# A two-norm transformer block on one core: the first pair of products written out by hand, with x turned by the host

## The chip, the cores and the metric

One core of one Trainium2 chip. A core has the engines PE (TensorE: matrix products, with its weight loads listed as PEld), DVE (VectorE: element by element), ACT (ScalarE), POOL (GpSimd) and SP (SyncE, which here only issues transfers), and 16 DMA engines that move data between HBM and the on-chip memory. The metric is device time in microseconds (us) of one execution; lower is better. All arithmetic on the data is in 32 bits.

## The reference

One layer on 512 tokens of width 2048, cut to what matters here:

```
h = rms_norm(x, norm1_g);  proj = h @ w_in         # columns qa ka va ra ga qb kb vb
A = chunked gated linear attention(qa, ka, va, gate from ga) ; out_a = rms_norm(A) * silu(ra)
B = dilated attention(rms_norm(qb), rms_norm(kb), vb)
x = x + concat(out_a, B) @ w_out
h2 = rms_norm(x, norm2_g)
x = x + (silu(h2 @ w_gate) * (h2 @ w_up)) @ w_down
```

## The kernel before

**Products.** All large products go by pairs: two weight blocks of 512 output columns are done together, as seven products P1 to P7 in place of eight (a scheme of sums and differences of quarters, as Strassen and Winograd do it). The left factor is the transposed x (or the transposed intermediate), in quarters r11, r21, r12, r22 of 256 features by 256 tokens; from them come the seven left operands A11, A12, A22, S1, S2, S3, S4. The right factor is in quarters named a, b, c, d; four products take a difference of two of them (`total` in the first pair, later `source`). Every operand is split into a high and a low part, since a product of full precision is made of three: ACT casts the high part (`wh`, `wl` is the low one, which DVE subtracts; for left operands `A...` the lines L174 and L175). A **unit** is one product for one group of 512 rows: 12 matrix instructions, 8 with `wh` and 4 with `wl`. A pair over 2048 rows is 28 units. There is one pair for qa and ka, four more on w_in, two on w_out, eleven on w_gate and w_up, six on w_down.

**The first pair** (`first_pair`, lines L384 to L492) differs from the rest. Nothing of x is on the chip when it starts. `LOADS` gives the order in which SP asks for x (16 pieces of 256 KB, rows as they lie in memory, `x_load`) and the weight quarters (512 KB each). PE turns x piece by piece (`x_turn`, L646: 64 transposes through `bank` in PSUM), and ACT (L658) or DVE (L653) scales the turned piece by the gain `g1` on its way into `xT`. The gains themselves arrive as rows and are turned by PE (`gains`, L566, L567), which needs the unit matrix `mats`. The lists `FIRST[i]` name what is put between the matrix instructions of unit i-2: `t` turns a piece, `+S1` to `+S4` add on DVE, `A..` and `S..` without a plus are splits, `sq` squares x on ACT for its norm (L621), `norm` finishes the norm, `gprep` makes the gate's weights from `gw` (POOL, ACT L735, DVE L736), `gate` are 32 of the gate's 64 small products (L753), and `seed` and `close` take a finished sum out of PSUM (L442 on ACT, L452 on DVE). A seed must be out before the next product adds to the same accumulator, and it needs the norm of x. The order on PE, ACT and DVE is exactly that of the program in this pair.

**The other pairs** come from `stream`. In each unit a `step` runs between the `wh` and the `wl` products: first what `later(n, ...)` has put off by n units, then one piece of the jobs in `background`. There the three engines' orders are set by a scheduler of the language from the order of the code, so neighbours may change places. A finished chunk of 512 columns is turned by `transposed_store` (PE L1071, ACT L1079 or L1082, then a store, L1086) and written to HBM: `mix_d` after the gate, `xn_d` after w_out, `p_d` after the gated product. The next stage loads it back by halves of 256 tokens (`part`, L1125; `fetch_part`, L1159). These buffers are laid out `[128, 2, 512]`, so that half a row is 1 KB.

Before the first pair on w_gate starts, A11 and S3 of all groups have to be in the program (`finish`). Groups 2 and 3 need the last chunks of w_out: `early_job` loads r11 and r21 of group 2 into `top`, splits A11, subtracts, splits S3, and then does the same for group 3.

A transfer that SP issues waits there for its data and for a free buffer, with all later transfers behind it.

## Time and profile before

| | |
|---|---|
| three runs | 1972.16, 1972.66, 1976.63 us; median 1972.66 |
| the profiled execution | 1970.3 us; its span, first to last instruction, 1968.5 us |
| busy, share of the span | PE 98%, PEld 85%, DVE 84%, ACT 55%, POOL 2% |
| moved | 294.49 MB read and 64.51 MB written, 182 GB/s over the span |
| mean granted PE clock | 0.997 |
| the first pair | 12.38 us (first product) to 105.30 us (first product of the next pair) |

Busy time is the union of an engine's instructions, so matrix instructions that overlap in the pipeline count once. The profile's rows give the start, the duration, the engine, the line, the operation, output and inputs, the count of merged instructions, and in square brackets how long the engine stood idle before it and who released it.

### The profile page before, as it was taken

How to read it: one execution, taken by the hardware profiler on the slowest of the kernel's cores; microseconds unless marked ns; L12 is line 12 of the kernel's file. 1: busy time of each engine (PE TensorE's matmuls, PEld its weight loads, DVE VectorE, ACT ScalarE, POOL GpSimd, SP SyncE). 2: the span in 40 equal slices, each digit the busy share in tenths (PEclk: the TensorE clock that was granted, in tenths of full speed). 3: DMA queues.
4: the chain of work that ended last, by engine and by line, in shares of the span. 5: the costliest groups of instructions: out<-in, count | busy, mean ns of one | idle time of the engine just before them, and what ended most of it. 6: DMA issues, size and time to landing. Idle time of an engine off the chain costs nothing.

```text
span 1968.5 us, 25771 instructions
## 1 busy us (share of the span) xinstructions
PE 1929.8 (98%) x9226; PEld 1669.3 (85%) x9226; DVE 1653.2 (84%) x1852; ACT 1086.9 (55%) x1586; POOL 47.4 (2%) x73
## 2 busy tenths in 40 slices
PE   7999999999999999999999999999999999999998
PEld 6888888888878878888888888888888888888887
DVE  7997778768789979878878878878879989989987
ACT  6664464566676656545545445545446646546443
POOL 0000130001000000000000000000000000000000
PEclk9999999999999999999999999999999999999999
DMA  7347364444566584443543453443545865855762
GB/s 278 113 174 270 103 203 151 150 163 159 191 225 213 189 273 161 171 172 128 179 169 134 172 171 124 172 167 126 176 166 164 288 211 180 302 180 181 243 214 75
DMA packets 183352, 358.34 MB, mean 182 GB/s; under 512 B 16070, under 2 KB 94735, under 8 KB 183224
## 3 DMA queue, kind: packets, MB, share of 16 engines
q1 hardware_dynamic: 183016, 356.62, 52.9%
q8 instruction: 72, 1.18, 0.2%
q14 instruction: 56, 0.46, 0.1%
q10 hardware_dynamic: 208, 0.08, 0.0%
HBM read 294.49 MB, written 64.51 MB: 182 GB/s over the span
## 4 chain that ended last, share of the span: by engine, by line
PE 71%; DVE 7%; DMA 4%; issue 2%; ACT 1%; SPq 1%; POOL 0%; DVEq 0%; ACTq 0%; POOLq 0%
PE acc L360 67%; DVE wl L334 2%; PE bank L1071 1%; DVE wa L255 1%; PE bank L956 1%; DMA k<-y_d 1%; PE bank L978 1%; DMA xn_d<-oT 1%; DVE AS L175 1%; ACT wh L330 0%; PE bank L971 0%; DVE seed L1249 0%; DVE seed L293 0%; PE bank L947 0%; DMA r<-mix_d 0%
## 5 line engine op out<-in xcount | busy, mean ns | idle before, releaser
L360 PE MATMUL acc<-wh,AS 128*128 128x512 f32 x3008 | 713.4, 380 | 1.8 <-DVE AS L175 1.0
L360 PEld LDWEIGHTS acc<-wh,AS 128*128 128x128 f32 x3008 | 567.7, 189 | 85.0 <-DVE AS L175 1.8
L330 ACT CAST wh<-wa 128x1024 fp32r<-128x1024 f32 x376 | 393.6, 1048 | 399.4 <-PE acc L360 367.6
L360 PE MATMUL acc<-wh,AA 128*128 128x512 f32 x2256 | 534.4, 380 | 5.8 <-ACT wh L330 5.8
L334 DVE TENSOR_TENSOR wl<-wa,wh 128x1024 fp32r<-128x1024 f32 x376 | 457.3, 1220 | 72.5 <-ACT wh L330 41.4
L360 PEld LDWEIGHTS acc<-wh,AA 128*128 128x128 f32 x2256 | 426.3, 189 | 68.5 <-ACT wh L330 8.1
L360 PE MATMUL acc<-wl,AS 128*128 128x512 f32 x1504 | 394.4, 384 | 6.1 <-DVE wl L334 5.9
L360 PEld LDWEIGHTS acc<-wl,AS 128*128 128x128 f32 x1504 | 279.4, 189 | 58.0 <-DVE wl L334 17.9
L360 PE MATMUL acc<-wl,AA 128*128 128x512 f32 x1128 | 296.8, 386 | 0.0
L360 PEld LDWEIGHTS acc<-wl,AA 128*128 128x128 f32 x1128 | 210.4, 190 | 31.2 <-DVE wl L334 1.9
L330 ACT CAST wh<-wb 128x1024 fp32r<-128x1024 f32 x94 | 98.5, 1048 | 120.4 <-PE acc L360 111.2
L330 ACT CAST wh<-wc 128x1024 fp32r<-128x1024 f32 x94 | 98.4, 1047 | 112.6 <-PE acc L360 106.2
L330 ACT CAST wh<-wd 128x1024 fp32r<-128x1024 f32 x94 | 98.6, 1049 | 105.0 <-PE acc L360 99.9
L334 DVE TENSOR_TENSOR wl<-wc,wh 128x1024 fp32r<-128x1024 f32 x94 | 114.7, 1221 | 39.7 <-ACT wh L330 39.4
L334 DVE TENSOR_TENSOR wl<-wd,wh 128x1024 fp32r<-128x1024 f32 x94 | 114.6, 1221 | 39.5 <-ACT wh L330 30.2
L255 DVE TENSOR_TENSOR wa<-wc,wa 128x1024 f32<-128x1024 f32 x94 | 114.6, 1223 | 37.0 <-DMA wc<-in_w_gate 21.0
L334 DVE TENSOR_TENSOR wl<-wb,wh 128x1024 fp32r<-128x1024 f32 x94 | 114.3, 1219 | 6.7 <-ACT wh L330 6.3
L255 DVE TENSOR_TENSOR wb<-wd,wb 128x1024 f32<-128x1024 f32 x94 | 114.6, 1219 | 0.5
L255 DVE TENSOR_TENSOR wa<-wb,wa 128x1024 f32<-128x1024 f32 x94 | 113.7, 1220 | 0.8
L255 DVE TENSOR_TENSOR wa<-wd,wa 128x1024 f32<-128x1024 f32 x94 | 113.1, 1218 | 0.1
L297 DVE SCALAR_TENSOR_TENSOR seed<-acc,rs,seed 128x512 f32<-128x512 f32 x96 | 70.6, 746 | 29.2 <-PE acc L360 29.2
L281 ACT ACTIVATE seed<-acc,rs 128x512 f32<-128x512 f32 x96 | 60.8, 682 | 3.1 <-DMA wc<-in_w_in 1.7
(276 smaller groups left out, 1347.4 us busy)
## 6 DMA issues: line engine op xcount, KB each, us to landing
wa<-in_w_gate SPq DMA_DIRECT2D x44, 512.0 KB, 3.6
wb<-in_w_up SPq DMA_DIRECT2D x44, 512.0 KB, 4.2
wd<-in_w_up SPq DMA_DIRECT2D x44, 512.0 KB, 4.2
wc<-in_w_gate SPq DMA_DIRECT2D x44, 512.0 KB, 3.4
wc<-in_w_in SPq DMA_DIRECT2D x28, 512.0 KB, 3.4
wa<-in_w_in SPq DMA_DIRECT2D x24, 512.0 KB, 4.9
wb<-in_w_in SPq DMA_DIRECT2D x24, 512.0 KB, 4.7
wd<-in_w_in SPq DMA_DIRECT2D x24, 512.0 KB, 5.2
```

Of the source, the lines that this page charges most:

```text
L175: nc.vector.tensor_tensor(a[:, :, 1, :], src, a[:, :, 0, :].bitcast(F32), op=ALU.subtract)
L255: nc.vector.tensor_tensor(src, self.quarter(one, g), src, op=ALU.subtract)
L281: nc.scalar.activation(halves(t), unfolded(src[m]), AF.Copy, scale=self.scale(half, m))
L297: nc.vector.scalar_tensor_tensor(halves(seed[m]), unfolded(src[m]), self.scale(half, m), halves(seed[m]), op0=ALU.mult, op1=ALU.add,)
L330: nc.scalar.copy(high[k], sources[k])
L334: nc.vector.tensor_tensor(low[k], sources.pop(k), high[k].bitcast(F32), op=ALU.subtract)
L360: nc.tensor.matmul(p.dst[prod][m], a[:, jj, hl, m * P : (m + 1) * P], folded(w[:, jj, :]), start=fresh and g == 0 and len(terms) == 2 and ...
L956: nc.tensor.matmul(lp[:, :n], qh[:, b * P : (b + 1) * P], kh[:, :n], start=True, stop=True)
L978: nc.tensor.matmul(op, vh[:, k, :], lgs[b][:, k * P : (k + 1) * P], start=(k == 0), stop=(k == b))
L1071: nc.tensor.transpose(bk[:, jj, m * P : (m + 1) * P], tiles[m][:, f : f + P], ident)
```

## The change

- **The first pair is written out.** `LOADS`, `FIRST`, `ON_VECTOR`, the planner `tokens`, `x_load`, `x_turn` and `gains` go. One list, `PLAN`, names every load (`D`) and every instruction of the pair in order. `h` and `l` are the high and low part of a right factor, `hi` and `lo` those of a left one, `+W` the difference of two weight quarters, `mH` and `mL` the 8 and the 4 matrix instructions of a unit, `rank` the gate's products, `x` the scaling by the gain.
- **The host hands over x transposed**, as `xt`, each quarter in 2 KB rows, and both gains by columns. PE turns nothing there; all 32 scalings are on ACT, in place, out of on-chip memory. x in rows is loaded too (`D.row`, 8 pieces of 512 KB), for the squares alone, which come 1024 wide: 8 in place of 16.
- `gw` is asked for ahead of the b quarters, and its preparation on POOL, ACT and DVE stands apart (`gp`, `gh`, `gl`). The take-out of P2 (`closea`) moves from the middle of the pair to behind its last unit.
- **Early loads together:** `early_job` takes a list of groups, asks for all their loads, and splits after that; used with both groups 2 and 3 ahead of the first w_gate pair.
- **Chunks turned later:** after the gate `later(1, ...)` becomes `later(2, ...)`, after w_out 2, or 3 for a pair's last chunk.
- **Contiguous halves:** `mix_d`, `xn_d`, `p_d` and `sums_d` become `[2, 128, 2, 256]`, so that a half is stored and loaded in 2 KB rows.

```
-LOADS = ("l0 l1 u0 u2 u6 l4 a0 u1 a1 u3 ...")   FIRST = (...)   ON_VECTOR = (...)
+PLAN = """
+D.r11.0 D.a.0 D.r11.1 D.a.1 D.r11.2 D.a.2 D.r11.3 D.a.3 D.r12.0 D.c.0 D.c.1 D.r12.3 D.r12.1
...
+mL.12 hi.S2.2 +S2.3 h.14 mH.13 lo.S2.2 hi.S2.3 +W.15 sq.3.0 mL.13 lo.S2.3 h.15 mH.14
...
-        def early(self, g, r11, r21):
-            pair_ = apool.tile([P, 2, 2, 256], F32, name=nm("top"), tag="A")
-            r11, r21 = r11(pair_[:, 0]), r21(pair_[:, 1])
-            yield
-            self.split("A11", g, r11)
...
+        def early(self, wanted):
+            got = []
+            for g, r11, r21 in wanted:
+                pair_ = apool.tile([P, 2, 2, 256], F32, name=nm("top"), tag="A")
+                got.append((g, r11(pair_[:, 0]), r21(pair_[:, 1])))
+                yield
+            for g, r11, r21 in got:
+                self.split("A11", g, r11)
...
-            store(dsts[b][:, :, half * 256 : (half + 1) * 256], d)
+            store(dsts[b][half], d)
...
-        later(1, lambda: transposed_store(
+        later(2, lambda: transposed_store(
...
-                    background.extend(early_job(opn, g, tops[g], False) for g in (2, 3))
+                    background.append(early_job(opn, [(g, tops[g]) for g in (2, 3)], False))
...
-            later(1, turn)
+            later(3 if which == 0 and half == 1 else 2, turn)
...
+            give("xt", a.reshape(2, 256, 8, 2, P).transpose(2, 0, 4, 3, 1))
```

**ACT at the start of the program.** `g` is the gain, `xT` a quarter of the transposed x, `AA` a left operand A11, `wh` the high part of a right factor. Before:

```order
L569 DMA q_93<-in_norm_g 16x128
L570 DMA mats<-in_mats 128x128
L571 DMA q_93<-in_norm_g 16x128
L658 ACTIVATE xT_159<-bank_286,g_88 128x256 x2
L174 CAST AA_36_300<-xT_160 128x2x256
L658 ACTIVATE xT_159<-bank_303,g_88 128x256 x2
L174 CAST AS_39_316<-xT_159 128x2x256
L174 CAST AA_41_325<-xT_159 128x2x256
L174 CAST AA_42_329<-xT_161 128x2x256
L408 CAST wh_332<-wa_116 128x1024
```

The same engine now:

```order
L581 DMA g_88<-in_g 128x16
L440 ACTIVATE xT_102<-xT_102,g_88 128x256 x2
L171 CAST AA_30_285<-xT_102 128x2x256
L465 CAST wh_287<-wa_229 128x1024
L440 ACTIVATE xT_104<-xT_104,g_88 128x256 x2
```

Two scalings and one cast now stand ahead of the first `wh`, in place of four scalings and four casts; the scaling no longer reads a PSUM bank that PE has filled.

**ACT ahead of the first seeds of the pair.** `L` and `ss` are the squares of x and their sums, `rs` the norm, `seed` the take-out of P1. Before:

```order
L635 ACTIVATE rs_104<-xms 128x2
L636 ACTIVATE rs_104<-rs_104 128x2
L174 CAST AS_120_732<-xT_161 128x2x256
L408 CAST wh_743<-wa_116 128x1024
L174 CAST AS_123_756<-xT_163 128x2x256
L621 ACTIVATE L_759,ss_100<-x_105 128x512
L442 ACTIVATE seed_761<-acc_353,rs_101 128x512
L442 ACTIVATE seed_763<-acc_354,rs_101 128x512
```

The same place now, where `x_464` is a piece of x in rows:

```order
L465 CAST wh_624<-wa_229 128x1024
L638 ACTIVATE rs_101<-xms 128x2
L639 ACTIVATE rs_101<-rs_101 128x2
L171 CAST AS_92_630<-xT_102 128x2x256
L171 CAST AS_93_632<-xT_104 128x2x256
L171 CAST AA_95_644<-xT_113 128x2x256
L625 ACTIVATE L_646,ss_97<-x_464 128x1024
L489 ACTIVATE seed_656<-acc_293,rs_98 128x512
L489 ACTIVATE seed_659<-acc_294,rs_98 128x512
```

In both orders the cast for unit 12 (`wh_743`, now `wh_624`) is ahead of the seeds, and unit 12 adds to the accumulators that they read. Three splits stand between the norm and the seeds in place of two, and the square between them is 1024 wide in place of 512.

**SP ahead of the first w_gate pair.** `xn_d` is the turned output of w_out, `top` the buffer of an early load. Before:

```order
L1086 DMA xn_d_205<-oT_6579 256x1x256
L1086 DMA xn_d_206<-PT_6588 256x1x256
L221 DMA wb_6903<-in_w_up 128x1024
L1125 DMA top_6592<-xn_d_205 128x2x256
L1159 DMA qT_6834<-xn_d_205 128x2x256
L1263 DMA x_d_197<-seed_6148 128x512
L1263 DMA x_d_198<-seed_6174 128x512
L1244 DMA q_6751<-in_x 128x512
L1244 DMA k_6754<-in_x 128x512
L1125 DMA top_6667<-xn_d_206 128x2x256 x2
```

Now:

```order
L1034 DMA xn_d_150<-oT_6507 128x512
L1034 DMA xn_d_151<-PT_6516 128x512
L222 DMA wd_6835<-in_w_up 128x1024
L1073 DMA top_6520<-xn_d_150 128x512
L1073 DMA top_6541<-xn_d_151 128x512 x2
L1211 DMA x_d_142<-seed_6048 128x512
L1211 DMA x_d_143<-seed_6074 128x512
```

The loads for group 3 (`top_6541`) follow at once on that for group 2, where five other transfers stood between; the stores themselves are issued one unit later.

## The prediction

> **What bounds the kernel now.** I read the busy shares first, then the busy time by stretches, then the order of time inside the stretches where PE is not full.

> ```profile
> PE 1929.8 (98%) x9226; PEld 1669.3 (85%) x9226; DVE 1653.2 (84%) x1852; ACT 1086.9 (55%) x1586; POOL 47.4 (2%) x73
> 5.50:12.40 6.90, 6.32 (x30) 5.71 (x30) 4.72 (x9) 4.76 (x10) 0.00 (x0) 1.00 1.04 349
> 12.40:30.50 18.10, 18.08 (x96) 15.57 (x97) 18.10 (x25) 15.88 (x31) 0.00 (x0) 1.00 1.05 390
> 30.50:36.50 6.00, 0.97 (x7) 0.63 (x5) 0.81 (x4) 1.19 (x3) 1.48 (x5) 0.92 0.99 281
> 36.50:43.40 6.90, 6.86 (x21) 5.73 (x22) 5.84 (x6) 4.76 (x10) 0.00 (x0) 0.57 0.55 202
> 43.40:105.30 61.90, 61.90 (x318) 55.13 (x316) 59.01 (x74) 43.39 (x77) 1.14 (x2) 1.00 0.38 137
> 1000.00:1900.00 900.00, 898.10 (x4213) 782.70 (x4212) 773.04 (x786) 469.55 (x554) 0.00 (x0) 1.00 0.54 187
> ```

> The columns behind the length are busy us of PE, PEld, DVE, ACT, POOL, then the granted PE clock, the share of the DMA engines and GB/s. In the long middle PE is full: of 900 us it lacks 1.9, so the 2 KB rows of `p_d` and the sums find nothing to shorten there. The first pair is another matter: PE does useful work only from 12.38, stands still for most of 30.5 to 36.5, then runs 6.9 us at a clock of 0.57, and in the last 62 us DVE is busy for 59.0, so it is as near the bound as PE.

> Why the gap at 30.5:

> ```profile
> 25.01 0.33 SPq L588 DMA_DIRECT2D k<-in_gw  x1
> 34.60 0.29 POOL L724 COPY v<-k 128x128 f32<-128x128 f32 x1 [33.49 <-DMA k<-in_gw]
> 35.16 0.85 ACT L735 CAST gs<-v 128x192 fp32r<-128x192 f32 x2 [6.64 <-POOL v L725]
> 36.54 1.12 PE L646 MATMUL bank<-mats,x 128*128 128x128 f32 x4 [5.07 <-DVE g L567]
> 39.16 3.50 PE L428 MATMUL bank<-wh,AA 128*128 128x512 f32 x8
> 63.86 1.89 PE L428 MATMUL acc<-wh,AS 128*128 128x512 f32 x8
> 66.45 1.89 PE L428 MATMUL acc<-wh,AS 128*128 128x512 f32 x8
> ```

> `gw`, issued at 25.01 behind all of x and the weights, lands 9.5 us later. POOL waits for it, ACT waits in its own order for POOL, and everything behind that on ACT, the casts for PE too, waits with it. After the gap a unit's first part takes 3.50 instead of 1.89 (pipelined). From 63.86, where unit 12 starts, to 66.45 one unit is 2.59 us, so 28 units are 72.5.

> The second place is where the first w_gate pair begins:

> ```profile
> 727.60:750.20 22.60, 16.39 (x70) 13.45 (x70) 17.76 (x26) 14.26 (x27) 0.00 (x0) 0.92 0.87 284
> 714.32 1.25 PE L1071 MATMUL bank<-mats,seed 128*128 128x128 f32 x8
> 718.37 0.90 SPq L1086 DMA_DIRECT2D xn_d<-oT  x1
> 725.59 0.57 SPq L1125 DMA_DIRECT2D top<-xn_d  x1
> 728.79 0.62 ACT L174 CAST AA<-top 128x512 fp32r<-128x512 f32 x1 [4.94 <-DMA top<-xn_d]
> 730.40 1.99 PE L360 MATMUL acc<-wh,AA 128*128 128x512 f32 x8 [2.73 <-ACT wh L330]
> 729.41 1.24 SPq L1125 DMA_DIRECT2D top<-xn_d  x2
> 735.44 0.62 ACT L174 CAST AA<-top 128x512 fp32r<-128x512 f32 x1 [2.15 <-DMA top<-xn_d]
> 737.05 1.99 PE L360 MATMUL acc<-wh,AA 128*128 128x512 f32 x8 [1.20 <-ACT wh L330]
> 741.05 0.33 PE L1071 MATMUL bank<-mats,q 128*128 128x128 f32 x1 [2.00 <-DVE q L1246]
> 742.61 2.05 PE L360 MATMUL acc<-wl,AA 128*128 128x512 f32 x4
> ```

> Five units and eight transposes, 14.0 us at full pace, take 22.6: 8.6 lost. ACT stands twice on a late `top`, for group 2 and again for group 3.

> **The change part by part.** *The start.* The first product waited for turned pieces; now for x, the gain, two scalings, a split and one cast:

> ```profile
> 12.38 1.99 PE L428 MATMUL acc<-wh,AA 128*128 128x512 f32 x8 [0.18 <-ACT wh L408]
> 5.56 0.26 PE L566 MATMUL bank<-mats,q 16*128 16x16 f32 x1 [5.56 <-DMA mats<-in_mats]
> DMA to landing us min/median/max: 3.7/5.0/7.6
> L658 ACT ACTIVATE xT<-bank,g 128x256 f32<-128x256 f32 x22 | 9.1, 473 | 5.0 <-PE bank L646 4.9
> L621 ACT ACTIVATE L<-x 128x512 bf16<-128x512 f32 x16 | 9.9, 624 | 0.0
> L442 ACT ACTIVATE seed<-acc,rs 128x512 f32<-128x512 f32 x8 | 5.0, 682 | 0.2 <-DVE rs L640 0.2
> ```

> A piece of x lands 3.7 us after an issue at 0.72 at the earliest (the landing row is that of x), and what ACT's queue brought (the unit matrix) was there by 5.56; I take 4.8 for x and gain, between 4.4 and 5.6. Then 2 x 0.41 (9.1 over 22) + 0.62 for a split + 1.03 for a cast (rows of ACT here and below) = 2.5, and PE starts at 7.3 (6.9 to 8.1) in place of 12.38.

> *The clock.* PE's transposes used to run before the first product, and it met the full pace (1.99 for 8). Now the first product is PE's first work. After the gap above, the mean clock of 0.57 over 6.9 us means half pace for 5.9 of them; a unit at half pace takes 5.2, so I charge one whole unit, 2.6 us more than its 2.59. [...]

> *Up to the first seeds.* Unit 12 adds to the accumulator of P1, so the seeds must be out. PE would be there at 7.3 + 12 x 2.59 + 2.6 + 3.8 for the first 32 gate products = 44.8:

> ```profile
> 47.68 3.94 PE L753 MATMUL bank<-AA,gs 128*128 128x256 f32 x32
> 46.83 1.03 ACT L408 CAST wh<-wa 128x1024 fp32r<-128x1024 f32 x1
> 47.76 0.62 ACT L174 CAST AS<-xT 128x512 fp32r<-128x512 f32 x1
> ```

> ACT has more to do by then: 32 scalings x 0.41, 18 splits, 13 casts, 5 squares of 1024 (about twice 0.62), 2 seeds, and small work of 1.1. An instruction starts about 0.1 before the last one ends (46.83 to 47.76), so 13.1 + 9.4 + 12.1 + 5.8 + 1.2 + 1.1 = 42.7, from 4.8 on: 47.5, and about 1.2 for early waits on PE: 48.7. All scalings being on ACT is what costs here: 32 against the 22 of before, though five DVE turns go. So unit 12 starts at 48.7, PE having waited 3.9.

> *To the end of the pair.* From 48.7, 16 units are 41.4 and the second gate products 3.6: 93.7. DVE's own list has to fit too:

> ```profile
> sum 99.80, PE 94.13 PEld 82.77 DVE 88.48 ACT 69.98 POOL 2.62; mean PE 18.83 PEld 16.55 DVE 17.70 ACT 14.00 POOL 0.52
> L653 DVE TENSOR_TENSOR xT<-bank,g 128x512 f32<-128x512 f32 x5 | 3.4, 686 | 1.7 <-PE bank L646 1.7
> L452 DVE SCALAR_TENSOR_TENSOR seed<-bank,rs,seed 128x512 f32<-128x512 f32 x2 | 1.4, 743 | 0.0
> 105.30 1.89 PE L360 MATMUL acc<-wh,AA 128*128 128x512 f32 x8
> ```

> From 5.5 to 105.3 it was busy 88.5. The five turns go (3.4), the gain copies (0.3), P2's take-out moves behind the pair (1.4), and about 0.9 of the next pair's work in this stretch: 82.5 are left. From a start at 6.2 that is 88.7 without a wait. PE's 93.7 is the larger; with 1.3 for waits between the two, the next pair starts at 95.0 instead of 105.3. Bounds: 89.6 (DVE's list without a wait, and four instructions of PE), and 100.2 (only the start is won, and the 92.9 from 12.38 to 105.30 stay). Gain 10.3 (5.1 to 15.7). P2's take-out then sits on DVE in the next pair, 1.4 that were done early; some of it shows, 0.5. The gap at 30.5 does not come back: `gw` is now asked for after 6 MB, 15 us at the 390 GB/s of 12.40 to 30.50, and `gp` and `gh` come after six units. The 4 MB of x in rows add 10 us of transfer at that rate; they go behind the b quarters, 12.6 MB in all by the last row that unit 12 needs: 32 us at that rate, from about 5 on, so 37.

> *The early loads and the late turn.* Transposes at 714.32 led to a usable `top` at 728.79, 14.5 later. The turn comes one unit later, 716.9, so `top` at 731.4. On ACT the split now stands behind one more cast for PE, so the unit held up is the next one, due at 727.67 + 2.59 = 730.3; the split and the cast make it 733.1, 2.8 late. That wait stays (2.73 now). What goes is the second one: group 3's loads are issued right behind group 2's, not 3.8 us later, so that ACT's second stop, PE's 1.20 and 2.00 and the slow clock after them (2.05 for four, about 1) go. Of 8.6 I take 4.0 as won. Bounds: 0, if the store and the loads land as late as the slowest above and the clock falls again; 8 if 2 KB rows shorten the 7.2 us store by a unit and more. SP issues the stores behind three weight loads either way.

> *The other late turns.* They remove waits such as PE's on `cr`, the gate's last chunk:

> ```profile
> PE bank L1071 <- DVE cr L1114: 1.4, 1, 1.4
> 580.00:640.00 60.00, 56.48 (x261) 46.63 (x262) 58.46 (x70) 40.97 (x64) 0.00 (x0) 1.00 0.59 197
> ```

> DVE is the next to be late there, busy for 58.46 of 60, so I count 0.5 of 1.4 (from -2 to 2).

> The sum: 10.3 - 0.5 + 4.0 + 0.5 = 14.3. The profiled execution took 1970.3 (span 1968.5), which gives 1956.0; the median of the runs shown, 1972.66, lies 2.4 above it, so **1958**.

> **The rivals.** *The clock stays low for longer.* PE starts among loads and casts that come one by one, and the row at 39.16 shows what a cold start costs. [...] Each further unit at half pace costs 2.6; 3.9 hide behind ACT's list before unit 12. Four more units would cost 10.4 - 3.9 = 6.5: 1964.5. Against it: at half pace a unit takes 5.2, and ACT's list gives 3.2 per unit (42.7 over 13), so PE would be full and warm up.

> *The late turn gives back what the joint loads win.* If group 2's load takes the 6 us that group 3's took (729.41 to 735.44) the wait reaches 5.7 and the clock falls, as at 36.5; nothing is won there, and the first w_out pair, whose chunks come a unit later too, loses that unit: 14.3 - 4.0 - 2.6 = 7.7, time 1965.

> *Slower: x in rows comes too late for the seeds.* Unit 12 can't start before the squares of tokens 0 to 255. If the DMA engines, already full (1.05), fall well below 390 GB/s with the 4 MB more, the last of these rows lands late; from 38 on, once ACT has reached it, each us costs one. The forecast's 14.3 are gone at a landing at 52.3, and at 58.2, 12.6 MB in 53 us or 238 GB/s, it is slower by 0.3%: 1979. No stretch above shows so low a rate while loads are queued.

> *It does not do what it says.* ACT's and PE's order might be worse than the sum: if the list makes DVE wait as in 30.5 to 43.4, only the start is won, and the boundary: 5.1 - 0.5 + 4.0 + 0.5 = 9.1, time 1964.

> **How the numbers follow.** The forecast holds 0.58, and a result still better than its bounds' middle (below 1950) 0.06; the low clock 0.13, the give-back 0.09, only the start 0.09, rows too late 0.05. The range takes the forecast's bounds, short of all ends falling on one side, and the three rivals that are faster than before: 1948 to 1968. One measurement of this kernel tells about 0.3% (5.9 us) from no change. Below 1966.7 lie the forecast, the better case and most of the three rivals: 0.86; within 0.3% the tails of these: 0.09; slower 0.05.

> **What would show it.** In the profile after: a first product near 7.3 at half pace for a unit; no idle time of PE over 2 us before unit 12, and one of about 4 there, ended by a seed on ACT; the next pair's first product near 95; at the first w_gate pair one wait on `top` in place of two. Wrong it would be if that first product comes after 100, or if PE waits on a landing of x.

## The result, and the profile after

The changed kernel takes 1959.32 us (median of 4 runs, 1958.01 to 1961.87) against 1972.41 before (4 runs, 1969.74 to 1976.63), a ratio of 0.9933 (95% interval 0.9912 to 0.9954). The profiled execution took 1958.01, its span 1956.1. Two more groups of runs, each on a chip of its own, gave 0.9942 (0.9929 to 0.9954) and 0.9957 (0.9945 to 0.9970).

Busy shares of the page, and busy time by stretches (the columns are those of the prediction):

```profile
PE 1918.2 (98%) x9160; PEld 1657.3 (85%) x9160; DVE 1648.0 (84%) x1845; ACT 1088.1 (56%) x1580; POOL 55.2 (3%) x73
5.00:12.00 7.00, 5.25 (x15) 4.30 (x16) 4.14 (x5) 6.11 (x10) 0.00 (x0) 1.00 1.04 399
12.00:30.00 18.00, 17.95 (x84) 15.38 (x82) 14.93 (x16) 17.54 (x35) 2.84 (x4) 1.00 1.02 368
30.00:45.00 15.00, 12.14 (x67) 10.24 (x68) 14.32 (x21) 14.41 (x29) 0.00 (x0) 1.00 1.03 407
45.00:95.00 50.00, 47.41 (x227) 39.55 (x226) 48.33 (x64) 32.64 (x49) 0.72 (x2) 1.00 0.50 175
1000.00:1900.00 900.00, 898.42 (x4216) 783.09 (x4215) 771.66 (x787) 470.27 (x554) 0.00 (x0) 1.00 0.54 189
```

The long middle is as full as before (898.42 of 900). The gap at 30.5 is gone, and PE works from 6.75, at half pace until 10.84. The order of time on PE in the first pair:

```profile
6.75 3.78 PE L421 MATMUL acc<-wh,AA 128*128 128x512 f32 x8 [6.75 <-ACT wh L465]
11.44 1.89 PE L421 MATMUL acc<-wh,AA 128*128 128x512 f32 x8
...
31.43 1.78 PE L421 MATMUL acc<-wh,AS 128*128 128x512 f32 x7 [1.48 <-DVE AS L174]
37.71 0.48 PE L421 MATMUL acc<-wh,AS 128*128 128x512 f32 x1 [1.05 <-ACT AS L171]
47.80 2.13 PE L421 MATMUL acc<-wh,AS 128*128 128x512 f32 x8
...
87.23 1.13 PE L421 MATMUL acc<-wl,AA 128*128 128x512 f32 x4 [0.64 <-DVE wl L473]
89.82 2.00 PE L421 MATMUL acc<-wh,AA 128*128 128x512 f32 x8 [1.46 <-ACT wh L465]
97.70 1.89 PE L358 MATMUL acc<-wh,AA 128*128 128x512 f32 x8
```

Unit 0 takes 4.69 (6.75 to 11.44), unit 12 starts at 47.80, and the next pair's first product comes at 97.70 instead of 105.30. At the first w_gate pair, on ACT:

```profile
719.18 0.62 ACT L161 CAST AA<-top 128x512 fp32r<-128x512 f32 x1 [4.26 <-DMA top<-xn_d]
721.50 0.62 ACT L161 CAST AA<-top 128x512 fp32r<-128x512 f32 x1 [0.23 <-DMA top<-xn_d]
```

Two waits on `top`, of 4.94 and 2.15, have become one of 4.26 and a rest of 0.23.

**Where the time went.** The order of units is the same in all kernels, so each unit's first product gives a lead: its start before minus its start in the kernel, from the profiled executions. A "fall" is a stretch of 3.4 us with a granted clock of 0.50 between the first warm stretch and the end of the work; it costs, by an estimate from these two numbers, at most 3.41 / 2 = 1.7. Pairs are counted behind the written one, as in the expectations: five more on w_in (not four, as said at the start), two on w_out, and pair 8 is the first w_gate pair. One run of turn_undone, of 2511 us at a mean granted clock of 0.753, is slow and left out.

| kernel | median, us | ratio to before (95%) | lead at pair 1 | pair 2 | pair 5, unit 18 | pair 8, unit 14 | end of span | falls: written pair / unit 18 of pair 5 to unit 14 of pair 8 / all |
|---|---|---|---|---|---|---|---|---|
| before | 1972.41 | | | | | | | 2 / 1 / 3 |
| changed | 1959.32 | 0.9933 (0.9912 to 0.9954) | 7.6 | 6.3 | 6.9 | 11.9 | 12.4 | 0 / 0 / 0 |
| after_again | 1963.16 | 0.9942 (0.9929 to 0.9954) | 6.7 | 5.1 | 3.4 | 8.7 | 8.5 | 0 / 0 / 1 |
| after_third | 1964.39 | 0.9957 (0.9945 to 0.9970) | 4.1 | 3.0 | 1.8 | 6.7 | 6.6 | 2 / 1 / 4 |
| late_undone | 1964.61 | 0.9963 (0.9953 to 0.9974) | 7.1 | 3.7 | 0.2 | 1.6 | 1.4 | 0 / 2 / 4 |
| turn_undone | 1963.21 | 0.9953 (0.9937 to 0.9969) | 5.0 | 3.4 | 0.9 | 6.3 | 6.1 | 1 / 0 / 2 |
| rows_undone | 1968.92 | 0.9981 (0.9969 to 0.9993) | 7.5 | 4.4 | 0.9 | 1.8 | -0.3 | 0 / 2 / 4 |
| rows_only | 1969.66 | 0.9981 (0.9971 to 0.9991) | -0.5 | -0.5 | -2.4 | -1.3 | -1.2 | 3 / 0 / 4 |
| no_plan | 1965.42 | 0.9963 (0.9949 to 0.9976) | 0.8 | 0.8 | 0.2 | 5.8 | 7.2 | 1 / 0 / 1 |
| gw_early | 1968.70 | 0.9979 (0.9969 to 0.9990) | 3.9 | 3.9 | 2.7 | 3.1 | 2.0 | 1 / 0 / 1 |
| warm | 1965.40 | 0.9955 (0.9939 to 0.9971) | 5.2 | 2.0 | -1.1 | 2.1 | 3.1 | 1 / 0 / 3 |
| sums_on_pool | 1988.45 | 1.0064 (1.0050 to 1.0079) | -17.5 | -19.4 | -22.3 | -18.1 | -18.0 | 6 / 0 / 7 |
| no_sums | 1963.08 | one run | 6.7 | 4.9 | 3.2 | 7.5 | 7.2 | 1 / 0 / 1 |
| filled | 1963.22 | 0.9954 (0.9941 to 0.9966) | 6.5 | 7.3 | 3.8 | 7.1 | 7.9 | 0 / 0 / 0 |

The gain of the changed kernel's profile has two places: the written pair, 7.6, and from the fifth to the eighth pair 11.9 - 6.9 = 5.0. From the ninth pair on nearly nothing moves. Of the 12.4, 5.1 are the three falls that the profile before has and this one has not; where a lead is told "without falls", 1.7 is added for each of the kernel's and taken off for each of before's.

### The profile page after: what moved, and what is told of

The parts are those of the page before. It is cut to its first block, busy times and chain, and to the rows that moved or that the text cites. A ratio compares the mean times of both kernels' runs of the same rounds, so it can differ in the third digit from the quotient of the medians.

```text
span 1956.1 us, 25599 instructions
## 1 busy us (share of the span) xinstructions
PE 1918.2 (98%) x9160; PEld 1657.3 (85%) x9160; DVE 1648.0 (84%) x1845; ACT 1088.1 (56%) x1580; POOL 55.2 (3%) x73
## 4 chain that ended last, share of the span: by engine, by line
PE 75%; DVE 6%; DMA 3%; issue 2%; ACT 1%; SPq 0%; POOL 0%; DVEq 0%; ACTq 0%
PE acc L358 71%; DVE wl L335 2%; PE bank L1019 1%; DVE wa L256 1%; PE bank L926 1%; PE bank L904 1%; DVE AS L162 1%; PE bank L919 0%; DMA xn_d<-PT 0%; DMA q<-y_d 0%; PE bank L895 0%; DMA q<-in_x 0%; DMA T<-p_d 0%; DMA r<-xn_d 0%; ACT wh L331 0%
## 5 line engine op out<-in xcount | busy, mean ns | idle before, releaser
L331 ACT CAST wh<-wb 128x1024 fp32r<-128x1024 f32 x94 | 98.6, 1049 | 123.8 <-PE acc L358 117.1
L331 ACT CAST wh<-wd 128x1024 fp32r<-128x1024 f32 x94 | 98.6, 1049 | 103.6 <-PE acc L358 98.5
```

The source lines that it names most:

```text
L331: nc.scalar.copy(high[k], sources[k])
```

## The experiments

**The late parts: early loads and turns.** Two kernels, the changed one with these edits (late_undone has both, turn_undone the first two alone):

```diff
-        later(2, lambda: transposed_store(
+        later(1, lambda: transposed_store(
-            later(3 if which == 0 and half == 1 else 2, turn)
+            later(1, turn)
-                    background.append(early_job(opn, [(g, tops[g]) for g in (2, 3)], False))
+                    background.extend(early_job(opn, [(g, tops[g])], False) for g in (2, 3))
```

> The changed kernel with the first pair and the contiguous halves kept, but the chunks turned one unit late everywhere and the early loads one group after another, as before. In the traces the changed kernel leads the kernel before by 6.7 us at unit 18 of the fifth pair and by 11.9 at unit 11 of the eighth. Theory: the late turns and the joint loads make that growth, so about 5 us are lost again: 1964.5 (1962.5 to 1967), and ACT stands twice on `top` at the first w_gate pair. Rival: the 2 KB rows make it (store and load of a chunk faster): 1959 to 1961, with one wait on `top` or two short ones.

> The changed kernel with the chunks turned one unit late as before, the joint early loads kept. Theory (the prediction's sizes): the joint loads win about 4 at the first w_gate pair and the other late turns 0.5, so this comes out at about 1960 (1958.5 to 1961). Rival: the late turns win most of the 5 us between the fifth and the eighth pair, as they take the transposes out from between DVE's or ACT's last work: 1963 to 1965, with PE waits on the chunk's tiles in the w_out pairs.

late_undone came to 0.9963, as the theory had it, against 0.9933 to 0.9957: 1 to 6 us of the gain go. From the fifth to the eighth pair it wins 1.4 where the changed kernel wins 5.0, 5.3 and 4.9 in its three profiles. ACT stands twice again:

```profile
726.73 0.62 ACT L161 CAST AA<-top 128x512 fp32r<-128x512 f32 x1 [4.89 <-DMA top<-xn_d]
734.06 0.62 ACT L161 CAST AA<-top 128x512 fp32r<-128x512 f32 x1 [2.83 <-DMA top<-xn_d]
```

Both stops are followed by a fall (at 729.8 and 740.0), so without falls it wins 1.4 + 3.4 - 1.7 = 3.1, near the 3.3, 3.6 and 4.9 of the changed kernel. In this profile, then, most of what the joint loads keep away is the half pace behind the two stops. turn_undone took 1963.21, the rival's time and not the theory's, but by its ratio (0.9953) it can't be told from the changed kernel, and it wins 5.4 from the fifth to the eighth pair. Only it wins in other places. From unit 18 of the fifth pair to unit 26 of the seventh (724.0 in the kernel before), the last one ahead of the boundary, it wins 0.6 where the changed kernel wins 2.7, 2.9 and 2.5; behind that unit it wins 4.8 against 2.3, 2.4 and 2.4. PE's wait on `cr`, 1.41 before, is 1.40 again in turn_undone and 0.24 in the changed kernel:

```profile
579.91 0.44 PE L1019 MATMUL bank<-mats,cr 128*128 128x128 f32 x2 [1.40 <-DVE cr L1062]
```
```profile
570.17 0.44 PE L1019 MATMUL bank<-mats,cr 128*128 128x128 f32 x2 [0.24 <-DVE cr L1062]
```

So in these profiles the late turns win some 2 us in the w_out pairs and give about as much back at the boundary, where `top` comes a unit later.

**The contiguous halves**, taken out of the changed kernel and put alone into the one before:

```diff
-    xn_d = [dram([2, P, 2, 256], f"xn_d{b}") for b in range(8)]
+    xn_d = [dram([P, 2, 512], f"xn_d{b}") for b in range(8)]
...
-            store(dsts[b][half], d)
+            store(dsts[b][:, :, half * 256 : (half + 1) * 256], d)
-            load(t, src[half])
+            load(t, src[:, :, half * 256 : (half + 1) * 256])
```

> The changed kernel with the chunks stored as before, 1 KB rows in halves of a 2 KB row; nothing else differs, the order on the four engines is the same. Theory of the prediction: nothing in the long middle, and at the first w_gate pair at most the landing of `top` (from its transposes to a usable `top` 14.5 us before and 11.6 in the changed kernel): about 3 us later there, of which PE loses 0 to 3: 1960.5 (1959 to 1962.5). Rival: rows change nothing at all there, since the loads in front set the landing: 1959.3 and 11.6 us again. Second rival: shorter rows cost in each of the 16 feed-forward pairs: over 1963.

> The kernel before with the contiguous halves alone; the order of PE, DVE, ACT and POOL is that of before. The changed kernel with this part undone came out 9.5 us slower by medians (0.9981 against 0.9933 of the kernel before), where the prediction had nothing for the long middle and at most a part of 4 at the first w_gate pair. Theory: rows of 2 KB alone win 4 to 9: 1963 to 1968, most of it before 760 us. Rival: most of those 9.5 were the stretches of half clock (four in that profile) and another chip: 1969 to 1972.

The change names `sums_d` as well, but that only gains a dimension of 1; its rows had 2 KB before. rows_undone lost most of the gain: 0.9981, 5 to 9.5 us more than the changed kernel by its three ratios, which is the second rival's time (over 1963). Group 3's loads follow at once on group 2's here too, and ACT's second stop on their landing is gone. But the first landing comes 13.6 us after its transposes (the changed kernel: 707.56 to 719.18, 11.6, and 12.7 and 11.9 in its other profiles). The next half's pieces, `r`, hold ACT for 2.94, which is not by the rows: in the changed kernel it is 2.40, 1.75 and 2.95.

```profile
729.06 0.62 ACT L161 CAST AA<-top 128x512 fp32r<-128x512 f32 x1 [5.84 <-DMA top<-xn_d]
731.05 0.61 ACT L161 CAST AA<-top 128x512 fp32r<-128x512 f32 x1
745.59 0.62 ACT L161 CAST AS<-r 128x512 fp32r<-128x512 f32 x1 [2.94 <-DVE r L1121]
```

Two falls (565.2 and 752.9) are in that stretch as well; without falls it wins 0.9 + 3.4 - 1.7 = 2.6. rows_only keeps 0.9981 of the time before: rows alone win 3.7 us (1.8 to 5.7), just under the theory's 4 to 9; by its time, 1969.66, it is in the rival's range, but before took 1973.49 on that chip. Its one profile, with four falls, lies 1.2 behind before's. So that 2 KB rows win is shown by the times of the runs; where they do, no profile settles. rows_undone lost 2.1 between the eighth pair and the end, rows_only nothing.

**Without the first pair.** The kernel before with the late turns, the joint early loads and the contiguous halves, that is with the edits of the two diffs above made on it:

> The changed kernel without the written first pair and the turned x: the kernel before with contiguous halves, joint early loads and late turns. So far, as shares of the kernel before: rows alone 0.9981, the changed kernel 0.9933 and 0.9942, without its late parts 0.9963. Theory A (the parts add up: rows 0.0019, late parts 0.0021 to 0.0030): 0.9955 to 0.9960, 1964 to 1965, and the first pair is worth 3 to 4 in the end, as much of the 6.7 to 7.6 that it leads by at its end is given back in the next pair. Theory B (what the first pair wins stays): 0.9975 to 0.9980, 1968 to 1969.

0.9963: nearer to theory A, just above its range. The rows' 0.0019 and the late parts' 0.0019 (late_undone's 0.9963 less 0.9944, the mean of the changed kernel's three ratios) add up to its 0.0037, and again 0.0019, some 3.7 us, are left for the written pair. Against after_third beside it alone (0.9957) the pair is worth 1 us, with intervals that overlap. But A's reason, that the pair's lead is given back in the next, covers 1.1 to 1.6; the rest is, by the two profiles, falls: after_third ends at 6.6 with four, no_plan at 7.2 with one.

**What the first pair's parts are worth.** The kernel before with `gw` asked for earlier:

```diff
-        name, i = what[0], int(what[1])
+        name, i = what[0], int(what[1]); what == "a2" and load(gaw, ins["gw"])
-        load(gaw, ins["gw"])
```

> The kernel before with one edit: gw is asked for in the middle of the early loads (ahead of a2) instead of behind all of them; nothing else differs. Theory: the gap at 30.5 is gw's landing alone, and it and the half pace after it cost PE about 9 us, of which DVE's list (59.0 busy of the 61.9 that follow) gives back a part: the next pair's first product at 98 to 101 instead of 105.3, and a time of 1966 to 1968.5. Rival A: another landing stands behind gw and the gap stays: 1972. Rival B: DVE's list sets the pair's end whole, so the gap goes and the end moves by under 2: 1971.

0.9979 (1968.70), and the next pair's first product 3.9 earlier, at 101.4: the theory, just short of its two ranges. The gap is gone (6.00 of 6.00, first row), but it comes back smaller: POOL waits 17.4 for `gq`, a small load behind the others, works on it for 8.93, and its clearing of `gs` waits behind that.

```profile
30.50:36.50 6.00, 6.00 (x33) 5.11 (x32) 6.00 (x9) 5.36 (x13) 1.52 (x1) 1.00 0.97 289
```
```profile
34.98 8.93 POOL L591 TENSOR_SCALAR gq<-gq 128x1 f32<-128x1 f32 x1 [17.40 <-DMA gq<-in_q_norm_g]
43.96 0.21 POOL L732 MEMSET gs<- 128x128 f32 x1
```
```profile
44.22 3.28 PE L753 MATMUL bank<-AA,gs 128*128 128x256 f32 x14 [2.51 <-POOL gs L732]
```

So one load moved in the old first pair brings half of the 7.6 that the new pair leads by, and nearly all of the 4.1 of after_third. In time its 0.0021 is no less than the 0.0019 that no_plan leaves for the whole written pair, though measured in another group. Next, the changed kernel with PE warmed up:

```diff
+        idle = mp.tile([P, 512], F32R, name="idle", tag="L", bufs=2)
+        nc.gpsimd.memset(idle.bitcast(F32), 0.0)
+        ib = bank()
+        for i in range(12):
+            nc.tensor.matmul(ib, idle[:, :P], idle, start=True, stop=True)
```

> The changed kernel with twelve products of a zeroed tile on PE ahead of the first unit, nothing else. It tells whether the half pace at the start (unit 0 takes 4.69 instead of 2.59) costs at the end of the first pair. If PE's start counts: the second unit starts about 2 earlier (9.4) and so does the next pair's first product (95.7), time lower by 2. Theory: DVE's list sets the pair's end (48.33 busy of 50 between 45 and 95), so the second unit starts at 9.4 and the next pair's first product stays at 97 to 98: the time of the changed kernel within 1.

The second unit starts at 9.93 instead of 11.44, and nothing of it is left at the end: PE only waits longer at unit 8 (2.3 for `AS`), falls to half pace at 34.9, and the pair ends 2.4 later than in the first profile, 1.4 later than in after_again beside it; the median is 2.2 above that one's. Without the fall it would end 0.3 ahead of after_again, so the cold start costs next to nothing at the pair's end. Whether DVE's list is the reason is what the next two were for: the twelve weight differences on POOL, then left out.

```diff
-                recent["dve"] = tt(s, q[one, g], s, op=ALU.subtract).ins
+                if k >= 12:
+                    nc.gpsimd.tensor_tensor(s, q[one, g], s, op=ALU.subtract)
+                else:
+                    recent["dve"] = tt(s, q[one, g], s, op=ALU.subtract).ins
```

> The changed kernel with the twelve weight differences of the first pair from unit 12 on computed on POOL instead of DVE (12 x 1.2 = 14 us of DVE's 48.33 between 45 and 95). Theory: DVE bounds that stretch, so PE's waits in it (2.6 us) go and the next pair's first product comes at 95 to 96 instead of 97.7, time lower by 1 to 2.6. Rival A: PE's waits there come from ACT and from the chain of single casts, nothing moves: 97.7. Rival B: POOL is so slow on 1024 columns or holds up DVE so much that the sources come late: after 99.

1.0064 (1.0050 to 1.0079): slower. POOL needs 2.3 to 3.3 us for one difference between 40.91 and 61.73 (two take 11.78 from 82.33 on), and DVE's small steps beside it stretch to over 2 us, so the norm comes late, and PE stands for a seed for 12.3 us (DVE, then POOL):

```profile
46.11 2.17 DVE L639 TENSOR_SCALAR xms<-xms 128x2 f32<-128x2 f32 x1
57.19 2.26 DVE L645 TENSOR_TENSOR nrs<-nrs,rs 128x2 f32<-128x2 f32 x1
74.43 0.17 DVE L639 TENSOR_SCALAR xms<-xms 128x2 f32<-128x2 f32 x1
```
```profile
45.76 2.50 POOL L461 TENSOR_TENSOR wa<-wd,wa 128x1024 f32<-128x1024 f32 x1
```

That is rival B, and it says nothing on the theory. The next kernel does:

```diff
-                recent["dve"] = tt(s, q[one, g], s, op=ALU.subtract).ins
+                if k < 12:
+                    recent["dve"] = tt(s, q[one, g], s, op=ALU.subtract).ins
```

> The changed kernel with the twelve weight differences of the first pair from unit 12 on left out (those products then use one quarter in place of a difference); all loads stay. DVE has 12 x 1.2 = 14 us less to do between 40 and 95, without POOL having any more. Theory: DVE sets that stretch (48.33 busy of 50), so the next pair's first product comes at 94 to 95.5 instead of 97.7 and 98.6, with under 1 us of PE waits from unit 12 on; PE's own list is next. Rival: the chain of single casts on ACT or PE's own list already set it: 97 to 98.5, the waits stay.

DVE is busy 37.45 of the 50 us in place of 48.33, and the next pair's first product comes at 98.6: not earlier. **DVE's busy time does not set the end of that pair.** PE is 0.7 ahead of the first profile at the unit of 83.95, and loses that and more, a fall too, at a stop on ACT:

```profile
45.00:95.00 50.00, 47.56 (x226) 40.80 (x225) 37.45 (x54) 32.22 (x48) 0.72 (x2) 0.97 0.58 202
```
```profile
87.38 0.69 ACT L490 ACTIVATE seed<-acc,rs 128x512 f32<-128x512 f32 x1 [5.63 <-DMA ka<-seed]
89.05 3.22 PE L421 MATMUL acc<-wh,AA 128*128 128x512 f32 x8 [2.35 <-ACT wh L466]
```

The same in the changed kernel, on ACT, on SP's queue and on DVE; then SP in no_sums, and the place of `closea` in the order before:

```profile
88.15 0.69 ACT L489 ACTIVATE seed<-acc,rs 128x512 f32<-128x512 f32 x1 [4.54 <-DMA ka<-seed]
88.74 1.03 ACT L465 CAST wh<-wa 128x1024 fp32r<-128x1024 f32 x1
```
```profile
77.87 4.94 SPq L222 DMA_DIRECT2D wa<-in_w_in  x4
84.28 0.98 SPq L1006 DMA_DIRECT2D ka<-seed  x2
```
```profile
83.50 1.41 DVE L497 SCALAR_TENSOR_TENSOR seed<-acc,rs,seed 128x512 f32<-128x512 f32 x2
```
```profile
81.11 0.98 SPq L1007 DMA_DIRECT2D ka<-seed  x2
```
```profile
71.81 1.40 DVE L452 SCALAR_TENSOR_TENSOR seed<-bank,rs,seed 128x512 f32<-128x512 f32 x2
```

`cpool` has six buffers, and seeds a, b and c fill them. Before, P2's take-out (`closea`) emptied a's at 71.81. Now `closea` stands behind all units, a's two buffers stay held, and `seedd.0` has to wait until the store of c's result, issued at 84.28, has landed. The cast that PE needs stands behind it. The wait is there in every profile with the new pair (4.54, 4.70 and 4.65 in the changed kernel, where after_again puts it down to DVE; 4.66 in late_undone) and there is none before. In no_sums that store is issued 3.2 earlier, at 81.11, but ACT goes on only 0.8 earlier, at 87.38: the landing holds it, not DVE. Whether DVE would be the next bound without that wait, no run shows. That two more buffers, an earlier `closea` or an earlier `closec` would take the wait away was not tried either; c's sum (P3) is complete at 73.8, behind unit 19, while `closec` stands on DVE at 83.50.

**The clock.** The changed kernel twice more, and once with two edits:

> The changed kernel once more, beside the others of this group. Its profile had no stretch of half PE clock between 10.84 and the end of the work, while those of the kernels with one part undone had one to four of 3.4 us each, each in the stretch of a 3.413 us grid behind one in which PE was busy for 0.44 or less (twice 0.65). Theory: such stretches come and go with where a PE wait of 1.5 to 2 us falls on that grid, so the same kernel has 0 to 3 of them, and its times spread by about 1.7 us for each: median 1960 (1958 to 1962), spread 4 or more. Rival: the changed kernel avoids them by its order: no half pace again, 1958 to 1959.5, spread under 2.

> The changed kernel a third time, as the base for the others of this group. In the second profile one half-pace stretch came at 471.9, behind a PE wait of 1.84 for q (PE busy 0.46 of the grid stretch before), in the first, where that wait was 1.54 (0.55), none. Expected: 0.994 of the kernel before (0.9933 and 0.9942 so far), 1960 to 1963.

```diff
+        if (h, lane) == (0, 0):
+            fb = bank()
+            for i in range(16):
+                nc.tensor.transpose(fb[:, :P], causal, ident)
...
+            if c0 == 0:
+                oh = rpool.tile([P, 2, 256], F32, name=nm("r"), tag="r")
```

> The changed kernel with two edits behind the first pair: sixteen transposes of a constant tile (1.7 us of PE at 0.11 each) ahead of the first transposes of q, where PE waits 1.5 to 2.0 for its landing; and the one-hot table loaded to a buffer that is free early, so that PE's wait of 1.1 to 1.4 for it at 136 goes. Theory: the half pace follows PE's idleness alone, so none comes at 472 to 477 although q lands no earlier (each cost 1.7), nor at 139: 1.5 to 3.5 less than the changed kernel in this group. Rival A: transposes don't count as work for the clock, or it follows something else: the half pace at 472 comes again. Rival B: the filler only delays q's transposes: later by up to 1.7 at unit 4 of the fifth pair and no gain.

after_again had one fall, at 471.9, and times from 1961.74 to 1965.09: the theory in kind, but 1 us above its range and with a spread of 3.4 for 4 or more. The wait for q stands in all 14 profiles, 1.54 to 2.25 us long; in eight a fall follows it, in six none. after_third, with four falls, came out above what was expected. filled gained nothing that shows (0.9954 to 0.9957), and its first edit missed: head 0's transposes run at 344, the wait at 470 is that of a later head. The second edit worked: no wait for the table, and the lead does not shrink in the next pair (6.5 to 7.3, where the changed kernel loses 1.1 to 1.6); it is lost later, 3.1 of it in the third pair, for a reason that I have not found. What the profiles do show is where the falls lie. Stretches of the 3.413 us grid around the wait for q, of after_third and then of filled:

```profile
470.29:473.70 3.41, 1.56 (x12) 1.33 (x13) 3.41 (x4) 1.15 (x2) 0.00 (x0) 1.00 0.90 295
473.70:477.11 3.41, 3.41 (x15) 3.05 (x13) 2.57 (x6) 2.39 (x6) 0.00 (x0) 0.50 0.06 16
```
```profile
465.98:469.39 3.41, 2.22 (x10) 1.28 (x8) 3.41 (x5) 1.86 (x3) 0.00 (x0) 1.00 0.30 99
469.39:472.80 3.41, 2.29 (x19) 2.06 (x19) 3.41 (x4) 1.65 (x3) 0.00 (x0) 1.00 0.92 271
472.80:476.21 3.41, 3.41 (x19) 2.86 (x18) 3.40 (x9) 2.59 (x6) 0.00 (x0) 1.00 0.41 117
```

In after_third 1.57 of a wait of 1.96 and one of 0.28 for `qT` lie in one stretch, PE is busy for 1.56 of 3.41, and the next stretch runs at 0.50. In filled a longer wait, 2.25, straddles a border, both stretches keep 2.2 or more, and the clock stays. In the first profile the wait of 1.54 left PE busy for 1.87 of its stretch (464.81 to 468.22), and no fall came: so the same program has a fall there in one profile and none in another. In these profiles a fall goes with where a wait lies on the grid, and not with its length alone. The falls explain the low lead of after_third's written pair: it has two in it (33.4 and 91.4, behind the waits at unit 8 and for `seedd`), and 7.6 - 2 x 1.7 = 4.2 is its lead of 4.1. The 6.7 of after_again, without a fall there, it does not explain.

The mean granted clock of each run is on record too, and (1 - clock) x time is an estimate of what the run lost to half pace. By means over the runs of a group the kernel before loses 6.6 to 7.6, after_again 3.9, after_third 5.5. What is gained over before beyond that loss is 6.6 and 7.1 for these two, 6.3 for turn_undone, 6.1 for late_undone, 5.4 for no_plan, 2.3 for rows_only, 2.1 for gw_early and 1.9 for rows_undone. The clock is given to 0.001, 2 us of a run, so about 1 us of each figure is uncertain. Read so, the 2 KB rows are the largest part (2.3 alone, 5 when taken out), the written pair is worth 1.7 beside no_plan, and most of what the late parts win is falls that don't come.

## Why the prediction was right, and where it was not

- **The start** was right as a chain: 6.75 for 7.3, in other profiles 6.66 to 7.28, mostly just below the bound of 6.9. x and the gain were there at 3.89 instead of 4.8, and the chain behind them took 2.9 instead of 2.5. **Half pace for a unit** too: 2.1 charged by the trace where I took 2.6; warm shows that the charge hides behind ACT's list, as the sum up to unit 12 assumed.
- **Unit 12** came at 47.80 for 48.7. What PE loses up to there was right, 4.0 for 3.9, and so was ACT's list: the first seed, started at 47.08, is out just ahead of that unit. But the sign "one of about 4 there, ended by a seed on ACT" did not show: PE's waits came earlier, the longest with 1.48 at unit 8 and 1.05 at unit 10, on splits.
- **The pair's end** was off: 97.70 for 95.0, 7.6 in place of 10.3, 6.7 and 4.1 in the repeats. The failed step is "PE's 93.7 is the larger; with 1.3 for waits between the two". DVE's list was not the other bound (no_sums). From 47.80 the 16 units (41.4) and the second gate products (4.9 in the trace, not 3.6) end at 94.1; of the 3.6 us that are left, 2.6 are the unit at 84.61, which takes 5.21 because ACT stands for `ka` (5.10 in no_sums, where PE does not wait for DVE in it). I had costed `closea` as 1.4 of DVE's time and missed that it holds two buffers. Its DVE cost was as said: the lead falls from 7.6 to 7.1 within four units. Of the 7.6, 3.4 are the two falls behind the old gap.
- **The boundary and the late turns** together were sized nearly right, 4.0 + 0.5 for 5.0, 5.3 and 4.9, of which 1.7 are the fall that before has there, and the two waits on `top` became one as described. The split was not: 2.3 to 2.4 at the boundary for 4.0, and 2.5 to 2.9 in the w_out pairs for 0.5. By turn_undone (4.8 and 0.6) the late turns win about 2 ahead of the boundary and cost as much there, so the rival "the late turn gives back what the joint loads win" came about in part, and that the sum of the two fits is luck.
- **The contiguous halves** had no term in the sum, by the step "the 2 KB rows of `p_d` and the sums find nothing to shorten there", and that failed. That the long middle is full was right, but not that nothing else waits for these rows: alone they win 3.7, and the changed kernel without them loses 5 to 9.5. I had them only in an upper bound at the boundary.
- **What I left out**: 1.1 to 1.6 in the next pair, by waits of 1.5 on `qT` and 1.1 on the one-hot table that before does not have; and chance. By the ratios rows alone, late parts and written pair bring about 3.7 each, where I had 0, 4.5 and 9.8. So the total of 14.3, which measured 13.1 here and 10.3 and 8.5 in the other groups, came out for partly other reasons than mine, and that 1958 lies so near to 1959.32 is in good part luck.
- **The rival "the clock stays low for longer"** came about in another place than it was put: at the start no further unit ran at half pace (the second takes 1.89 for its first eight), but falls came later, as in after_third from 473.70, behind its wait of 1.96 for q. "x too late" did not show: no wait of PE ended on x.

Open: where the 2 KB rows win, how much of the written pair stays in the end (1 to 6 us, by the group and by the falls), and why the same two kernels gave 0.9933 to 0.9957 in three groups; between the last two the granted clock makes up the difference (6.6 and 7.1 beyond it).

## What to carry to other kernels

A take-out moved to the end keeps its buffers as well as its time: before moving it, count who allocates from the same pool behind it, and which store has to land first. Where a stretch shows two engines nearly full, take work off one of them before calling it the bound; here 11 us off DVE moved nothing, as ACT still stood for a store's landing. One profile of a kernel that is full of PE holds some us of chance, three falls of the clock here and none there, so a sum made against one profile is checked against several, or without the falls.

## What the runs showed of the hardware

```profile
734.77 0.56 SPq L1034 DMA_DIRECT2D xn_d<-oT  x1
```
```profile
725.47 0.32 SPq L1034 DMA_DIRECT2D xn_d<-oT  x1
```
